# Feed-forward joints of a hybrid decoder layer: when the last rows' steps, operand loads, weight sums and next weights are issued

## The chip, the cores and the metric

The kernel runs on one NeuronCore of one Trainium2 chip. The metric is the device time of one execution in microseconds (us); less is better. In the profile PE is the matrix engine TensorE and PEld its weight loads, DVE is VectorE, ACT is ScalarE, POOL is GpSimd, and SP is the engine whose queue issues nearly all DMA transfers here.

## The reference

One decoder layer over a prompt of 2048 tokens and 8 x 8 sample tokens, D = 1024, D_FF = 4096, all in float32:

```python
h = rms_norm(x, g_mix_pre)                       # attention (window 128) and gated linear attention
mix = jnp.einsum('bte,ed->btd', jnp.concatenate([attn, gla_out], axis=-1), w_out)
x = x + rms_norm(mix, g_mix_post)
h = rms_norm(x, g_ffn_pre)
u = jax.nn.relu(jnp.einsum('btd,df->btf', h, w_up))
f = jnp.einsum('btf,fd->btd', u * u, w_down)
x = x + rms_norm(f, g_ffn_post)
```

The change concerns the last four lines, the feed-forward part, and its seams.

## The kernel before

**Numbers.** Every float32 operand is split into a high and a low part (`split_copy`, `split_by`: ACT writes the high part, DVE subtracts it from the source to get the low part), and each product is three matmuls (high x high, high x low, low x high).

**Feed-forward as seven products.** The prompt's 16 row tiles of 128 tokens form two superblocks (`sb` = 0, 1) of 8. Each matrix product is cut into quarters, and seven products of sums of quarters, numbered p = 1 to 7, take the place of eight. For `up` the sums of the tokens' quarters are the tensors H1 to H7 (from `ht`, kept in DRAM as `h_d`, loaded as `hraw`, split by `load_h`); the sums of w_up's quarters are made on the chip by DVE (`sums_13`, `sums_24`, tiles `t13`) and split (`split_sums`: `s130`, `s131`, `s240`, `s241`; `split_up`: `w00` to `w11`). For `down` the sums of the hidden quarters are stored in DRAM as `s_d`, and those of w_down are made during the first `up` by `sum_down` (four subtractions of 128x256 and a store to `t_d`).

**The stages.** After the out projection, whose last row tile (15) goes through `residual` (scale, add, second norm, transpose `xnT`, quarters' sums), come, for each superblock, `up(sb, fc)` for 16 chunks `fc` of 256 hidden columns, 7 products of 12 matmuls 128x512 each, and `down(sb)`: seven passes in the order `DOWN_ORDER`, each of 16 units of 12 matmuls. For `sb` = 0 products 0, 8 and 9 of each chunk are the sample's (`sam`, `both`, `fold`). In a unit, `down_operand` loads `rs` (from `s_d`) and `rt` (from `t_d` or w_down) and splits them into `o0s`, `o1s`, `o0t`, `o1t`; the raw tiles have two buffers, the split ones three. At a pass's end `gather` adds the four banks `dn` into the output tiles `f`, and at the end `finish` norms and stores a row tile.

**What sets the order.** `te`, `ac` and `dv` are in-order wrappers of PE, ACT and DVE: what is recorded through them (line L136) runs in the order of the code. Other instructions are placed among them by a scheduler. SP's queue is in order; a DMA there waits for its own semaphores and holds up all behind it. The first chunk has an order of its own, `UP_FIRST` = (1, 0, 2, 8, 5, 7, 9, 6, 3, 4); the others use `UP_ORDER` = (1, 5, 7, 0, 6, 3, 8, 2, 9, 4).

**Names and places.** "The first chunk" is (0, 0), the joint of out projection and feed-forward. Its operands H7, H6, H3, H4 are fetched one by one just ahead of their products:

```python
if first and p in H_LATE[1:]:
    if p != 7:
        fetch_h(0, p, "t" if p == 6 else "h")
    run(load_h(0, p))
```

`sum_down(fc - 1, 1)` stands behind product 1 of chunk `fc`, `sum_down(fc, 0)` behind the last product of chunk `fc`, and the last one, `sum_down(NFC - 1, 1)`, behind the last chunk. The weights of chunk (1, 0) are loaded and split after `down(0)`.

## Time and profile before

| | us |
|---|---|
| median of 3 runs (lowest, highest) | 2359.76 (2357.86, 2364.57) |
| profiled execution, its own time | 2353.07 |
| its span, first to last instruction | 2351.3 |
| PE busy in the span | 2245.4 |
| DVE busy | 1607.7 |
| ACT busy | 1202.8 |

The profiled execution lies 6.7 us below the median of the runs. PE is busy for 95% of the span, so that 106 us of it are time in which PE does nothing; 1.8 us of the profiled time lie outside the span. The granted clock of PE is 0.987 of full speed on the mean. Of an engine's row the last bracket is the idle time ahead of it and what ended that.

### The profile page before, as it was taken

To read this page: it belongs to the slowest core of one execution; us is meant where nothing else is said; L and a number is where in the kernel's file an instruction comes from. 1 tells how busy PE (TensorE), PEld (TensorE's weight loads), DVE (VectorE), ACT (ScalarE), POOL (GpSimd) and SP (SyncE) were. 2 spreads that over 40 slices of the span, in tenths; PEclk is the share of its full clock that TensorE was granted. 3 is DMA by queue.
4 is the path that set the end of the run, shared out by engine and by line. 5 is a ranking of instruction groups with operands and counts; after the bars stand their busy time and mean duration, and the time that the engine had idled before them with its cause. 6 is when DMAs were issued, how large, how long until landed. Compare 5 with 4: busy or idle time off the path is not lost.

```text
span 2351.3 us, 34131 instructions
## 1 busy us (share of the span) xinstructions
PE 2245.4 (95%) x11800; PEld 1885.6 (80%) x11800; DVE 1607.7 (68%) x3343; ACT 1202.8 (51%) x2513; POOL 271.5 (12%) x428
## 2 busy tenths in 40 slices
PE   8999999999999999889999999999989999999998
PEld 7888887888888788678888878888768888888886
DVE  5888868777777765677777765454676666545557
ACT  5787755345545444455555554333445555444444
POOL 3566412111121100000000000000000000000000
PEclk9999999999999999999999999999989999999999
DMA  6343231121112456676666786655744443666666
GB/s 226 125 147 120 97 115 46 64 70 50 46 46 90 141 178 207 208 262 232 233 236 241 245 287 215 190 177 162 241 141 150 150 150 146 217 223 191 195 194 213
DMA packets 226546, 391.86 MB, mean 167 GB/s; under 512 B 22865, under 2 KB 134886, under 8 KB 222262
## 3 DMA queue, kind: packets, MB, share of 16 engines
q1 hardware_dynamic: 226054, 389.56, 49.7%
q8 instruction: 93, 1.52, 0.3%
q14 instruction: 79, 0.65, 0.1%
q10 hardware_dynamic: 320, 0.13, 0.0%
HBM read 255.08 MB, written 135.59 MB: 166 GB/s over the span
## 4 chain that ended last, share of the span: by engine, by line
PE 69%; DVE 18%; ACT 5%; DMA 5%; issue 3%; POOL 1%; SPq 0%; DVEq 0%; ACTq 0%; POOLq 0%
PE dn L136 22%; PE uc L136 7%; PE ua L136 7%; PE out L1228 7%; PE gproj L136 5%; PE ue L136 4%; PE ud L136 4%; PE ub L136 3%; DVE AT L988 2%; DMA rt<-t_d 2%; DVE s L136 2%; DVE XQ L967 2%; PE proj L136 2%; DVE before L982 1%; PE sam L136 1%
## 5 line engine op out<-in xcount | busy, mean ns | idle before, releaser
L136 PE MATMUL dn<-o0t,o0s 128*128 128x512 f32 x896 | 352.1, 393 | 6.5 <-ACT o0t L222 6.0
L136 PE MATMUL dn<-o1t,o0s 128*128 128x512 f32 x896 | 353.5, 395 | 3.8 <-DVE o1t L223 3.5
L136 PE MATMUL dn<-o0t,o1s 128*128 128x512 f32 x896 | 351.9, 393 | 0.0
L223 DVE TENSOR_TENSOR o1s<-rs,o0s 128x512 fp32r<-128x512 f32 x224 | 154.7, 691 | 223.8 <-ACT o0s L222 211.8
L136 PE MATMUL gproj<-wg,gx 128*128 128x388 f32 x1408 | 288.5, 352 | 0.0
L222 ACT ACTIVATE o0s<-rs 128x512 fp32r<-128x512 f32 x224 | 141.3, 631 | 282.1 <-PE dn L136 236.1
L136 PEld LDWEIGHTS gproj<-wg,gx 128*128 128x128 f32 x1408 | 245.0, 190 | 8.6 <-issue 4.5
L136 PEld LDWEIGHTS dn<-o0t,o0s 128*128 128x128 f32 x896 | 168.9, 189 | 47.0 <-ACT o0t L222 9.4
L136 PEld LDWEIGHTS dn<-o1t,o0s 128*128 128x128 f32 x896 | 168.9, 189 | 46.2 <-DVE o1t L223 9.6
L136 ACT ACTIVATE st<-st 128x512 f32<-128x512 f32 x224 | 141.1, 630 | 123.1 <-DVE st L136 119.1
L136 PE MATMUL uc<-H,s 128*128 128x512 f32 x768 | 194.4, 401 | 9.9 <-ACT s L1423 8.8
L136 PEld LDWEIGHTS dn<-o0t,o1s 128*128 128x128 f32 x896 | 169.1, 189 | 35.4
L136 PE MATMUL ua<-H,w 128*128 128x512 f32 x744 | 184.1, 396 | 6.7 <-ACT w L1423 4.3
L223 DVE TENSOR_TENSOR o1t<-rt,o0t 128x512 fp32r<-128x512 f32 x224 | 153.8, 687 | 49.0 <-ACT o0t L222 48.6
L136 PEld LDWEIGHTS uc<-H,s 128*128 128x128 f32 x768 | 146.3, 191 | 47.6 <-ACT s L1423 9.6
L222 ACT ACTIVATE o0t<-rt 128x512 fp32r<-128x512 f32 x224 | 139.3, 622 | 66.2 <-DMA rt<-t_d 40.7
L136 PEld LDWEIGHTS ua<-H,w 128*128 128x128 f32 x744 | 140.6, 191 | 38.9 <-ACT w L1423 5.1
L1228 PE MATMUL out<-wo,mt 128*128 128x512 f32 x680 | 160.9, 395 | 0.2 <-DVE x L1359 0.2
L212 POOL TENSOR_TENSOR frs<-rs_v,half 128x1 f32<-128x1 f32 (+1 forms) x13 | 8.9, 698 | 1311.7 <-DVE rs_v L210 726.4
L1228 PEld LDWEIGHTS out<-wo,mt 128*128 128x128 f32 x680 | 126.5, 188 | 28.8 <-DVE x L1359 0.6
L136 DVE TENSOR_TENSOR st<-st 128x512 f32<-128x512 f32 x160 | 110.8, 692 | 54.9 <-ACT st L136 51.6
L136 PE MATMUL proj<-wa_hi,xh 128*128 128x384 f32 (+1 forms) x272 | 96.1, 357 | 0.6 <-ACT wa_hi L136 0.6
(368 smaller groups left out, 4283.6 us busy)
## 6 DMA issues: line engine op xcount, KB each, us to landing
s_d<-st SPq DMA_DIRECT2D x32, 1792.0 KB, 9.1
rs<-s_d SPq DMA_DIRECT2D x224, 256.0 KB, 2.8
raw<-in_w_up SPq DMA_DIRECT2D x64, 512.0 KB, 5.1
rt<-t_d SPq DMA_DIRECT2D x128, 256.0 KB, 3.2
rt<-in_w_down SPq DMA_DIRECT2D x96, 256.0 KB, 3.0
t<-in_w_down SPq DMA_DIRECT2D x64, 256.0 KB, 3.7
t_d<-t SPq DMA_DIRECT2D x32, 512.0 KB, 8.1
gx<-xt_d SPq DMA_DIRECT2D x28, 512.0 KB, 4.3
```

Source lines behind the costliest of these rows:

```text
L136: ins = call(*a, **k)
L212: nc.gpsimd.tensor_tensor(out, v[:n], e, op=ALU.pow)
L222: nc.scalar.activation(hi, src, AF.Copy)
L223: vector.tensor_tensor(lo, src, f32(hi), op=ALU.subtract)
L967: nc.vector.tensor_tensor(xq[rr, :, l, r, : n // 2].rearrange("p g (m b) -> p g m b", b=b), dr[rr], qr[rr], op=ALU.mult)
L982: nc.vector.tensor_tensor(br, br, bl[..., b - 1 :].to_broadcast(list(br.shape)), op=ALU.add)
L988: nc.vector.copy_predicated(dst, m, gm.rearrange("p h (m b) -> p h m b", b=b))
L1228: te.matmul(p_, x, w[:, cc], start=k + u == 0, stop=k == KT - 1 and u == len(products) - 1)
```

## The change

Nothing is computed in another way except that `down` takes its passes in another order, with the additions in `gather` to match (as many as before). The rest is when things are issued:

- The last row tile's `residual` is a generator, `last_rows`, whose steps run between the products of the first chunk, and each operand load has a fixed place there (`opening`). `s130` and `s131` of the first chunk are made before that tile's steps, the w_up loads of chunk (0, 1) go out at once, and the tile's `xnT` transposes and its four `ht` subtractions move behind products 7 and 6. A pool `keep` on the left side lets those tiles share memory with later ones.
- `sum_down` runs twice in a chunk from chunk 2 on, behind products 1 and 2, and a third time (behind product 4) in chunks 4, 6, 8 and 10, so that none is left behind the last chunk.
- In `down(0)` the loads of the second superblock's H are in the first three and a half passes; `finish` of the first four row tiles comes one pass earlier; at the start of the last pass the weights of chunk (1, 0) are loaded, summed and split (`ahead_of_up`); `finish` of the other four row tiles runs inside chunks (1, 0) and (1, 1).

```diff
-DOWN_ORDER = (6, 1, 5, 7, 2, 3, 4)
-H_EARLY, H_LATE = (1, 2), (5, 7, 6, 3, 4)
+DOWN_ORDER = (6, 1, 5, 3, 2, 7, 4)
+DOWN_SUMS = (4, 6, 8, 10)
+H_FETCH = ((6, 0), (6, 8), (1, 0), (1, 8), (5, 0), (5, 8), (3, 0))
+H_EARLY, H_LATE = (1, 2), (5, 7, 6, 4, 3)
...
-    def residual(i, banks, vector=nc.vector):
+    def residual(i, banks, tensor=nc.tensor, scalar=nc.scalar, vector=nc.vector):
...
+        def ahead(kind):
+
+            if last:
+                return
+            if kind == "a":
+                split_up(sb, fc + 1, 0, ac, dv)
+            elif kind in ("13", "24"):
+                split_sums(sb, fc + 1, int(kind), ac, dv)
+            else:
+                (sums_13 if kind == "s13" else sums_24)(sb, fc + 1, dv)
+
+        def downs(p):
+
+            if sb == 0 and fc > 1 and p in ((1, 2, 4) if fc in DOWN_SUMS else (1, 2)):
+                sum_down(*next(down_halves))
...
+    def opening(p, taken, ahead):
+
+        if p == 1:
+            taken(p)
+            split_sums(0, 0, 13, ac, dv)
+        elif p == 0:
+            next(last_rows)
+        elif p == 2:
+            taken(p)
+            next(last_rows)
+            fetch_h(0, 3, "t")
+        elif p == 8:
+            taken(p)
+            run(load_h(0, 7, ac, dv))
+            fetch_h(0, 6, "tmp")
+        elif p == 5:
+            taken(p)
+            sums_24(0, 0, dv)
+            split_sums(0, 0, 24, ac, dv)
+            fetch_h(0, 4, "raw")
+            run(load_h(0, 6, ac, dv))
+            U.pop("tmp").release()
+        elif p == 7:
+            taken(p)
+            next(last_rows)
+        elif p == 9:
+            taken(p)
+            close_pools(R)
+            for q in H_LATE[3:]:
+                h_pools[q] = open_pool(f"h_{q}")
+            run(load_h(0, 3, ac, dv))
+        elif p == 6:
+            run(load_h(0, 4, ac, dv))
+            ahead("a")
+            taken(p)
+            run(last_rows)
             load_up(0, 2)
             for half in range(2):
                 load_down(0, half)
-        if sb == 0:
-            sum_down(fc, 0)
-        dv.tensor_tensor(s[:, 6], s[:, 0], s[:, 6], op=ALU.subtract)
-        dv.tensor_tensor(s[:, 5], s[:, 3], s[:, 6], op=ALU.subtract)
-        dv.tensor_tensor(s[:, 4], s[:, 5], s[:, 0], op=ALU.add)
-        if sb == 0:
-            sample_features(fc, sam)
-
-        def end():
-            dv.tensor_tensor(s[:, 1], s[:, 1], V, op=ALU.add)
-            yield
-            squared(s[:, 1])
-            dv.tensor_tensor(s[:, 2], s[:, 1], s[:, 5], op=ALU.subtract)
-            nc.sync.dma_start(s_d[sb][fc], s)
-
-        return end()
+        elif p == 3:
+            ahead("s13")
+            ahead("13")
+        else:
+            ahead("s24")
+            ahead("24")
...
-                if sb == 0 and not first:
-                    sum_down(fc - 1, 1)
...
-        if sb == 0:
-            sum_down(fc, 0)
...
+    def ahead_of_up():
+
+        open_pools(U, ("ah", "al", "t13", "s13h", "s13l", "s24h", "s24l"), "u1")
+        load_up(1, 0)
+        yield 1.4
+        split_up(1, 0, 0)
+        yield 0.7
+        sums_13(1, 0, nc.vector)
+        yield 1.4
+        split_sums(1, 0, 13, nc.scalar, nc.vector)
+        yield 1.3
+        sums_24(1, 0, nc.vector)
+        yield 1.4
+        split_sums(1, 0, 24, nc.scalar, nc.vector)
+        yield 1.3
...
+            if (sb, p, fc) == (0, late, 0):
+                deque(chain.from_iterable(todo), 0)
+                for name in ("fa", "smp", "fs"):
+                    Dp.pop(name).release()
+                weights = ahead_of_up()
+                next(weights)
+                todo.extend((*waiting, weights))
...
-                if p == 3 and sb == 0:
-                    todo.append(finish(NB, f[NB]))
-                if p == 3 or p == late:
-                    todo.extend(finish(i, f[i]) for i in range(sb * 8 + 4 * (p == late), sb * 8 + 4 * (p == late) + 4))
-                if p == 3 and sb == 1:
+                if p == 2:
+                    if sb == 0:
+                        todo.append(finish(NB, f[NB]))
+                    todo.extend(finish(i, f[i]) for i in range(sb * 8, sb * 8 + 4))
...
+    last_rows = residual(*early.pop(0), te, ac, dv)
+    sums_13(0, 0, dv)
+    run(load_h(0, 5, ac, dv))
+    load_up(0, 1)
+    next(last_rows)
     for sb in range(NSB):
...
-            load_up(sb, 0)
-            split_up(sb, 0, 0)
-        sums_13(sb, 0, nc.vector)
-        split_sums(sb, 0, 13, nc.scalar, nc.vector)
-        sums_24(sb, 0, nc.vector)
-        split_sums(sb, 0, 24, nc.scalar, nc.vector)
-        if sb:
-            split_up(sb, 0, 1)
-        load_up(sb, 1)
-        end = iter(())
+            open_pools(U, ("raw", "bh", "bl", "st0"), "u1")
+            load_up(sb, 1)
+        end, ends = iter(()), iter(())
         for fc in range(NFC):
-            end = up(sb, fc, end)
+            if sb and fc < 2:
+                ends = chain.from_iterable(rows_left[2 * fc : 2 * fc + 2])
+            if sb and fc == 1:
+                Dp.pop("fbA").release()
+                open_pools(U, ("st1",), "u1", "right")
+            end = up(sb, fc, end, ends)
+            run(ends)
```

The first place is DVE in the first chunk. `ht_11` is the last rows' sum tile, `st_0_0` the first chunk's hidden quarters, `H31`, `H61`, `H41` are low parts of operands, `s131_0_1` and `w01_0_1` low parts of the next chunk's weights. Before:

```order
L136 TENSOR_TENSOR ht_11_11026<-ht_11_11026 128x512
L223 TENSOR_TENSOR H31_0_11281<-hraw_0_3_0_11276,H30_0_11280 128x1024
L1424 TENSOR_TENSOR s131_0_0_11139<-t13_0_0_11135,s130_0_0_11138 128x1024
L223 TENSOR_TENSOR H31_0_11281<-hraw_0_3_2_11278,H30_0_11280 128x1024
L1469 TENSOR_TENSOR t13_0_0_11135<-t13_0_0_11135,raw0_0_0_10812 128x4x128
L1470 TENSOR_TENSOR t13_0_0_11135<-raw1_0_0_10813,t13_0_0_11135 128x4x128
L1424 TENSOR_TENSOR s241_0_0_11145<-t13_0_0_11135,s240_0_0_11144 128x1024
L136 TENSOR_TENSOR t13_0_1_11171<-raw0_0_1_11148,raw1_0_1_11149 128x4x128
L136 TENSOR_TENSOR t13_0_1_11171<-raw0_0_1_11148 128x4x128
L136 TENSOR_TENSOR w01_0_1_11183<-raw0_0_1_11148,w00_0_1_11182 128x1024
L136 TENSOR_TENSOR st_0_0_11152<-st_0_0_11152,ud_0_0_11156 128x512
L136 TENSOR_TENSOR s131_0_1_11243<-t13_0_1_11171,s130_0_1_11242 128x1024
```

After:

```order
L138 TENSOR_TENSOR H31_0_11248<-hraw_0_3_0_11158,H30_0_11247 128x1024
L138 TENSOR_TENSOR H31_0_11248<-hraw_0_3_2_11160,H30_0_11247 128x1024
L138 TENSOR_TENSOR H41_0_11266<-hraw_0_4_0_11201,H40_0_11265 128x1024
L138 TENSOR_TENSOR H41_0_11266<-hraw_0_4_2_11203,H40_0_11265 128x1024
L138 TENSOR_TENSOR w01_0_1_11272<-raw0_0_1_11089,w00_0_1_11271 128x1024
L138 TENSOR_TENSOR st_0_0_11121<-st_0_0_11121,ua_0_0_11106 128x512
L138 TENSOR_TENSOR st_0_0_11121<-st_0_0_11121 128x512
L138 TENSOR_TENSOR ht_11_11026<-ht_11_11026 128x512 x4
L138 TENSOR_TENSOR st_0_0_11121<-st_0_0_11121,uc_0_0_11105 128x512
L138 TENSOR_TENSOR t13_0_1_11307<-raw0_0_1_11089,raw1_0_1_11090 128x4x128
L138 TENSOR_TENSOR t13_0_1_11307<-raw0_0_1_11089 128x4x128
L138 TENSOR_TENSOR s131_0_1_11311<-t13_0_1_11307,s130_0_1_11310 128x1024
```

The `ht` subtractions have gone from ahead of the first chunk's weights to a place between H4's split and the next chunk's sums; the next chunk's `s131_0_1` now stands behind H6, H3, H4, `w01_0_1` and them.

The second place is SP's queue at the end of the first `up`. `t_d15_147<-t_15_1` is the store of w_down's last sums, `rs_0_6_n` and `rt_0_6_n` the operands of unit n of the first down pass, `s_d0_15` the last chunk's store. Before:

```order
L1621 DMA rs_0_6_3_14128<-s_d0_3_103 128x512
L1621 DMA rt_0_6_3_14134<-t_d3_135 128x512
L1397 DMA hraw_1_5_2_14487<-h_d1_99 128x1024
L1607 DMA sm_d_148<-samp_15_13991 128x256
L1621 DMA rs_0_6_4_14152<-s_d0_4_104 128x512
L1621 DMA rt_0_6_4_14158<-t_d4_136 128x512
L1589 DMA s_d0_15_115<-st_0_15_13843 128x3584
L1500 DMA t_d15_147<-t_15_1_13876 512x1x256
L1621 DMA rs_0_6_5_14176<-s_d0_5_105 128x512
```

After:

```order
L1414 DMA hraw_1_7_0_14508<-h_d1_99 128x1024
L1515 DMA t_d15_147<-t_15_1_13821 512x1x256
L1718 DMA rs_0_6_2_14113<-s_d0_2_102 128x512
L1718 DMA rt_0_6_2_14119<-t_d2_134 128x512
L1718 DMA rs_0_6_3_14137<-s_d0_3_103 128x512
L1718 DMA rt_0_6_3_14143<-t_d3_135 128x512
L1704 DMA sm_d_148<-samp_15_13993 128x256
L1785 DMA smp_0_0_14315<-sm_d_148 128x8x128
L1718 DMA rs_0_6_4_14161<-s_d0_4_104 128x512
L1718 DMA rt_0_6_4_14167<-t_d4_136 128x512
L1640 DMA s_d0_15_115<-st_0_15_13874 128x3584
L1718 DMA rs_0_6_5_14185<-s_d0_5_105 128x512
```

That store has moved from just ahead of unit 5's operands to ahead of unit 2's; half a load of sample features (`smp_0_0`) has come in ahead of unit 4's.

The third place is DVE at the end of `down(0)`. `t13_1_0`, `s131_1_0` and `s241_1_0` are the sums of chunk (1, 0)'s weights and their low parts; `f_4` to `f_7` are output tiles of `finish`. Before, behind the last pass:

```order
L210 TENSOR_SCALAR rs_v_17101<-fssq_4_17097 128x1
L1424 TENSOR_TENSOR w01_1_0_17196<-raw0_1_0_17191,w00_1_0_17195 128x512
L1651 SCALAR_TENSOR_TENSOR f_4_14472<-f_4_14472,frs_4_17100,gfpost0_14058 128x1024
L210 TENSOR_SCALAR rs_v_17113<-fssq_5_17109 128x1
L210 TENSOR_SCALAR rs_v_17125<-fssq_6_17121 128x1
L1632 TENSOR_TENSOR f_4_14472<-f_4_14472,fx1_4_17095 128x1024
L1651 SCALAR_TENSOR_TENSOR f_5_14474<-f_5_14474,frs_5_17112,gfpost0_14058 128x1024
L1651 SCALAR_TENSOR_TENSOR f_6_14476<-f_6_14476,frs_6_17124,gfpost0_14058 128x1024
L210 TENSOR_SCALAR rs_v_17137<-fssq_7_17133 128x1
L1462 TENSOR_TENSOR t13_1_0_17199<-raw0_1_0_17191,raw1_1_0_17192 128x4x128
L1651 SCALAR_TENSOR_TENSOR f_7_14478<-f_7_14478,frs_7_17136,gfpost0_14058 128x1024
L1424 TENSOR_TENSOR s131_1_0_17203<-t13_1_0_17199,s130_1_0_17202 128x1024
```

After, at the seam of the last two passes (units (7, 13) to (4, 0)):

```order
L225 TENSOR_TENSOR o1t_0_7_13_16634<-rt_0_7_13_16632,o0t_0_7_13_16633 128x512
L225 TENSOR_TENSOR o1s_0_7_14_16652<-rs_0_7_14_16650,o0s_0_7_14_16651 128x512
L225 TENSOR_TENSOR o1t_0_7_14_16658<-rt_0_7_14_16656,o0t_0_7_14_16657 128x512
L1439 TENSOR_TENSOR s131_1_0_16914<-t13_1_0_16886,s130_1_0_16913 128x1024
L1484 TENSOR_TENSOR t13_1_0_16886<-t13_1_0_16886,raw0_1_0_16750 128x4x128
L225 TENSOR_TENSOR o1s_0_7_15_16676<-rs_0_7_15_16674,o0s_0_7_15_16675 128x512
L225 TENSOR_TENSOR o1t_0_7_15_16682<-rt_0_7_15_16680,o0t_0_7_15_16681 128x512
L225 TENSOR_TENSOR o1s_0_4_0_16700<-rs_0_4_0_16698,o0s_0_4_0_16699 128x512
L1485 TENSOR_TENSOR t13_1_0_16886<-raw1_1_0_16751,t13_1_0_16886 128x4x128
L225 TENSOR_TENSOR o1t_0_4_0_16706<-rt_0_4_0_16704,o0t_0_4_0_16705 128x512
```

The sums and the low part `s131_1_0` now stand among the operand splits some 16 units before the end of `down(0)`, no longer behind the `finish` of four row tiles.

## Rows read from the trace of the kernel before

**Rows 1.** The page, part 1: busy us (share of the span) and instructions of each engine.

```profile
PE 2245.4 (95%) x11800; PEld 1885.6 (80%) x11800; DVE 1607.7 (68%) x3343; ACT 1202.8 (51%) x2513; POOL 271.5 (12%) x428
```

**Rows 2.** Windows: length, then busy us (instructions) of PE, PEld, DVE, ACT, POOL; PEclk, DMA share, GB/s.

```profile
976.00:1021.00 45.00, 30.01 (x123) 23.34 (x122) 32.30 (x42) 22.93 (x34) 1.44 (x2) 0.77 0.83 267
...
1021.00:1043.00 22.00, 22.00 (x106) 18.26 (x105) 19.72 (x33) 11.79 (x21) 0.00 (x0) 1.00 0.72 249
...
1350.00:1375.00 25.00, 19.70 (x73) 14.72 (x72) 14.29 (x25) 11.40 (x21) 0.00 (x0) 0.86 0.92 308
...
1640.00:1674.00 34.00, 33.02 (x144) 26.69 (x142) 24.05 (x36) 19.36 (x33) 2.50 (x4) 1.00 0.61 194
...
1696.00:1740.00 44.00, 33.11 (x114) 24.36 (x113) 30.55 (x41) 17.15 (x26) 3.67 (x4) 0.84 0.47 156
```

**Rows 3.** Timeline of PE around the first chunk: start, us, group, idle before and releaser.

```profile
983.44 1.11 PE L136 MATMUL sam<-w,xsT 128*128 128x256 f32 x8
...
987.27 1.15 PE L1375 MATMUL xnT<-ident,x 128*128 128x128 f32 x8 [2.72 <-DVE x L136]
...
993.69 1.22 PE L136 MATMUL uc<-H,s 128*128 128x512 f32 x2 [5.27 <-ACT s L1423]
...
1006.18 1.11 PE L136 MATMUL sam<-fold,both 128*128 128x64 f32 x4 [4.02 <-ACT both L136]
...
1023.74 0.63 PE L136 MATMUL uc<-H,s 128*128 128x512 f32 x2
```

**Rows 4.** Timeline of ACT, SP's queue and DVE in the first chunk.

```profile
991.33 1.06 ACT L222 ACTIVATE H<-hraw 128x1024 fp32r<-128x1024 f32 x1 [1.42 <-DMA hraw<-h_d]
...
1003.65 1.06 ACT L136 ACTIVATE w<-raw 128x1024 fp32r<-128x1024 f32 x1 [4.62 <-DMA raw<-in_w_up]
...
984.99 2.48 SPq L1397 DMA_DIRECT2D hraw<-h_d  x2
...
997.19 2.71 SPq L1420 DMA_DIRECT2D raw<-in_w_up  x2
...
1005.15 0.69 DVE L136 TENSOR_TENSOR t<-raw,raw 128x512 f32<-128x512 f32 x1 [4.86 <-DMA raw<-in_w_up]
...
1006.36 1.22 DVE L136 TENSOR_TENSOR w<-raw,w 128x1024 fp32r<-128x1024 f32 x1
```

**Rows 5.** Timeline of DVE, SP's queue and PE at the start of the first down pass.

```profile
1360.23 0.42 DVE L136 TENSOR_TENSOR t<-t 128x256 f32<-128x256 f32 x1
...
1360.67 0.57 SPq L1500 DMA_DIRECT2D t_d<-t  x1
...
1361.30 0.73 SPq L1621 DMA_DIRECT2D rs<-s_d  x1
...
1368.55 0.80 PE L136 MATMUL dn<-o0t,o0s 128*128 128x512 f32 x1 [4.45 <-ACT o0t L222]
...
1374.02 0.40 PE L136 MATMUL dn<-o0t,o0s 128*128 128x512 f32 x1
```

**Rows 6.** Timeline of PE from the last down pass into the second up.

```profile
1702.40 0.74 PE L136 MATMUL ua<-H,w 128*128 128x512 f32 x2 [0.22 <-ACT w L1423]
...
1705.02 4.09 PE L136 MATMUL ua<-H,w 128*128 128x512 f32 x10 [1.88 <-DVE w L1424]
...
1712.67 1.22 PE L136 MATMUL uc<-H,s 128*128 128x512 f32 x2 [3.56 <-ACT s L1423]
...
1731.36 0.73 PE L136 MATMUL ua<-H,w 128*128 128x512 f32 x2 [4.05 <-ACT w L1423]
...
1739.21 2.90 PE L136 MATMUL ua<-H,w 128*128 128x512 f32 x12
...
1758.69 1.54 PE L136 MATMUL ua<-H,w 128*128 128x512 f32 x6
```

**Rows 7.** Timeline of PE in the last down pass, unit 7.

```profile
1674.35 0.50 PE L136 MATMUL dn<-o1t,o0s 128*128 128x512 f32 x1 [1.32 <-DVE o1t L223]
```

**Rows 8.** The page, part 6: a store of w_down's sums, median us to landing.

```profile
t_d<-t SPq DMA_DIRECT2D x32, 512.0 KB, 8.1
```

More of the change, by code (lines that the diff above doesn't have):

```diff
@@ L238, in three @@
         engine.matmul(ps, lh, rl, start=False, stop=False)
-        engine.matmul(ps, ll, rh, start=False, stop=last)
+        return engine.matmul(ps, ll, rh, start=False, stop=last)
     gcol = cpool.tile([P, KT], F32, name="gcol")
@@ L1506, in squared, with up, s, product @@
         ac.activation(t, t, AF.Square)
[L1508 to L1514 removed]
+    def up(sb, fc, before, steps=iter(())):
+        first, last = (sb, fc) == (0, 0), fc == NFC - 1
         X, Z, Y, V = (bank([P, BT], kind, f"u{kind}_{sb}_{fc}") for kind in ("ab"[first], "c", "ba"[first], "de"[fc % 2]))
         sam = bank([P, BT], "b", f"sam_{fc}") if sb == 0 else None
+        place = []
+        def s(n):
+            if not place:
+                pool = keep if (sb, fc % 2) == (0, 1) else U[f"st{fc % 2}"]
+                place.append(pool.tile([P, 7, BT], F32, tag="st", name=f"st_{sb}_{fc}", bufs=1))
+            return place[0][:, n]
+        def product(p):
+            out = {1: X, 2: X, 5: Z, 3: Z, 7: V, 4: V, 6: Y}[p]
+            hi, lo = H[p]
+            for k in range(KT // 2):
+                for u, (a, b) in enumerate(((0, hi), (0, lo), (1, hi))):
+                    te.matmul(
+                        out, weight(sb, fc, p, a, k), b[:, k], start=p in (1, 5, 7, 6) and k + u == 0,
+                        stop=k == KT // 2 - 1 and u == 2, skip_group_check=True,
+                    )
+        def add(out, a, b, op=ALU.add):
+            dv.tensor_tensor(s(out), a, b, op=op)
+        def taken(p):
+            if p == 1:
+                ac.activation(s(1), X, AF.Copy)
+            elif p == 5:
+                ac.activation(s(3), Z, AF.Copy)
+            elif p == 7:
+                add(3, s(3), V)
+            elif p == 6:
+                add(1, s(1), Y)
+                add(3, s(3), s(1))
+                squared(s(3))
+            elif p == 2:
+                squared(s(0), X)
+            elif p == 8:
+                both.append(U["sam"].tile([P, FC], F32, tag="sam", name=f"both_{fc}", bufs=1))
+                ac.activation(both[0], sam[:, :FC], AF.Copy)
+            elif p == 9:
+                for u in range(2):
+                    te.matmul(
+                        sam[:, FC + u * NS : FC + (u + 1) * NS], both[0][:, u * P : (u + 1) * P], fold, start=True, stop=True
+                    )
+        both = []
+        def ahead(kind):
[10 more added lines that the diff above has]
+                sum_down(*next(down_halves))
@@ L1712, in gather @@
             yield 0.7
-        elif p == 3:
-            add(fa[:, two], fa[:, two], p_)
-            yield 0.7
+        elif p == 7:
+            for dd in (two, one):
+                add(fb[:, dd], fb[:, dd], p_)
+                yield 0.7
         else:
@@ L1777, in down @@
             del parts[n]
-            if n == NFC // 2 and sb == 0:
-                smp = load_sample(0)
-            if fc == 8 and sb == 0:
-                todo.append(load_h(1, H_ORDER[DOWN_ORDER.index(p)]))
+            if n == 8:
+                with tc.issue_after(done.ins):
+                    for part in range(2 * (sb == 0)):
+                        load_sample(0, part)
+                    gains_post(sb)
+            if p == 5 and sb == 0 and fc in (8, NFC - 1):
+                load_sample(1, fc // 9)
```

238 lines of the change are left out of this document (129 added, 109 removed).

## The prediction

> **What bounds the kernel now.** I read the busy times first: PE works in 95% of the span, DVE in 68% and ACT in 51% [rows 1]. The sum of PE's work is not touched by this change, so only the 106 us in which PE stands still, and the time in which it runs at less than full clock, can be had. Then I read the windows by stage. In a steady chunk of the first up PE is busy throughout (22.00 of 22.00), with DVE at 19.72 [rows 2]. Three stretches are different: the first chunk with 30.01 of 45.00, the start of the first down pass with 19.70 of 25.00, and the way from the last down pass into the second up with 33.11 of 44.00; together 15.0 + 5.3 + 10.9 = 31.2 us idle. In each the granted clock also drops, to 0.77, 0.86 and 0.84 on the mean [rows 2]. [...] Last, PE's timeline says who ended each wait there.
>
> A product of 12 matmuls takes 19.48 / 7 = 2.78 us (seven of them between 1739.21 and 1758.69) [rows 6]. After the wait of 4.45 us one unit of 12 took 1374.02 - 1368.55 = 5.47 us [rows 5]. So a wait is paid again, by 2.7 us, where the clock has fallen during it.
>
> **First chunk.** From the end of the sample's second product (984.55) to the second product of chunk (0, 1) at 1023.74 lie 39.2 us [rows 3]. Full-clock work in it: five products and one of the next chunk, 16.7 us, transposes 1.15, the fold some 0.4: 18.2 us. So 21.0 us are lost. The long waits: 2.72 for the last rows' norm on DVE, 5.27 for `s130` on ACT, 4.02 for `both` on ACT [rows 3]. The last is a queue: `both` stood behind a weight split that had waited 4.62 us for w_up loads, issued only at 997.19 [rows 4].
>
> The change makes `s130` and `s131` ahead of the last rows' steps, so product 5 follows without a wait, and issues those w_up loads at the start, so that `both` has nothing late ahead of it. What is late next? DVE. I follow its new order (first place in the change). The last rows' norm ended at about 987.2 (the transposes begin then); one more low part (1.22) now stands ahead of it: 988.4. H7's low parts follow, 2 x 1.22, to 990.9, so product 7 waits some 3 us. H6's two loads share H7's memory and go out as H7's halves are split, the first at about 989.7. A load of this kind issued at 984.99 was first used at 991.33, 6.3 us later; with ACT's 1.06 H6's first low part starts at 997.1 [rows 4]. From there DVE is a chain without a gap: H6 2.44, one hidden sum 0.69, H3 2.44, H4 2.44, `w01_0_1` 1.22, two sums 1.38, four `ht` subtractions 2.76, one sum 0.69, two weight sums 1.38, ACT's `s130_0_1` 1.06, `s131_0_1` 1.22: 17.7 us (1.22 for 1024 columns, 0.69 for 512 [rows 4]). It ends at 1014.8, where the third matmul of chunk (0, 1)'s second product needs it; before, that matmul ran at about 1024.2. Gain: 9.4 us, not 21. Upper bound: back to back these additions start 0.61 apart (1005.15 and two of them to 1006.36), a tenth off the DVE part: 11.1. Lower bound: the products behind H6 are three, and one of the next chunk; at the low clock each takes 5.47, so 997.3 + 21.9 = 1019.2, gain 5.0. I take 9.4, because with two of the four at low clock PE is done at 997.3 + 16.5 = 1013.8, still ahead of DVE.
>
> [...]
>
> **Start of the first down pass.** PE waits 4.45 us for unit 5's operands, whose load left SP at 1361.30, right behind the store of w_down's last sums at 1360.67, and that waited for DVE's last sum, begun at 1360.23 [rows 5]. In the new order (second place) this store is ahead of unit 2's loads, its sums having been made within chunk 15. Unit 5's load then waits for its buffer, that is for unit 3's split, which needs unit 0 to be through. Counting back five units from the stop at 1364.1 the pass begins at about 1349.3 (the other 0.85 us of idle time taken off); unit 0 ends at 1352.1, splits follow, issue near 1354. Even with the 8.1 us of a store [rows 8] a load issued then lands by 1362.1, a little before it must be split. Gain 4.45 + 2.7 = 7.2. Bounds: 0 if another transfer takes the place of the store, 8.0 with the 0.85.
>
> The price is paid in the chunks: 32 `sum_down` of 4 x 0.42 us are only moved, none is added [rows 5]. Four chunks have three instead of two: 19.72 + 1.7 = 21.4 of 22 us on DVE, still covered. Each store must land (8.1 [rows 8]) before the next load into that half may pass SP: three make 24.3 us in a chunk of 22, two make 16.2 in the next, so a delay of some 2 us is caught up. I take 0; if it were not caught up, 4 x 2.3 = 9.
>
> **Into the second up.** Chunk (1, 0) runs from 1702.40 to 1739.21, 36.8 us, where a chunk takes 19.48: 17.3 lost, with waits of 1.88 for DVE's `w01`, 3.56 for ACT's `s130` and 4.05 for ACT's `w10` [rows 6]. All of them are weights loaded after the pass and split behind the `finish` of four row tiles. Now sums and splits are made in the last two passes (third place); only `w10` and `w11` remain, needed five products later, 14 us. What is late next is chunk (1, 1): its loads leave at the end of the pass, and DVE has four gathers 2.8, five sums of 512 columns 3.5, two low parts and six full-row steps of `finish` 9.8, and half a `w01` 0.7 before chunk (1, 1) can start: 16.8 us, begun 2 us ahead of the pass's end, against 19.5. Covered by some 4 us; I still take 1 us off for the waits on GpSimd between these steps: 16.3. If that cover is gone, PE waits and the clock falls once more: 16.3 - 4 - 2.7 = 9.6 as lower bound.
>
> The cost lies in the pass before the last. DVE works 24.05 of 34.00 us in a stretch of the old last pass in which four row tiles are finished [rows 2], and there PE once waited 1.32 us for a split [rows 7]. The same finish now comes a pass earlier, with four weight sums, a half `w01` and a low part between: 2.8 + 0.7 + 1.2 = 4.7 us more. The old stall goes, a new one comes: between +1.3 (it just fits) and -4.7 + 1.3 = -3.4 (nothing fits); I take -1.
>
> **Sum.** 9.4 + 7.2 + 16.3 - 1 = 31.9 us off the profiled execution's 2353.07: 2321.2. The median of the runs shown is 6.7 us above that execution, so 2327.9, about 2328, and by the bounds of the terms 2322 (11.1 + 8.0 + 17.3 + 1.3 = 37.7) to 2349 (5.0 + 0 + 9.6 - 3.4 = 11.2). Less than 0.3%, 7.1 us, is not to be told from no change.
>
> **The rivals.**
>
> *The first chunk keeps the low clock* (chance 0.14): gaps of 1 to 3 us remain ahead of products 7 and 6. For it speaks the 0.77 of the stretch, against it that DVE and not PE ends last there. Gain 5.0 or nothing in place of 9.4: 2332 to 2337.
>
> *DVE becomes the bound in the last two passes and chunk (1, 0)* (0.12): 9.6 - 3.4 in place of 15.3: 2337. For it speaks the 1.32; against it the fewer `finish` steps in the last pass.
>
> *The joint of the first down pass does not open* (0.08): unit 5 waits for its load as before, behind half a load of sample features and the last chunk's store; gain 0 there: 2335.
>
> *Slower* (0.05): in the first up `sum_down` now stands in DVE's in-order queue ahead of the next chunk's low parts. If the loads it waits for come late through SP, DVE stands as it once stood 4.86 us for w_up [rows 4]; it has 2.3 us to spare in a chunk. In 14 chunks that is 14 x 2.6 = 36 us, which just eats the gain; from 5.2 us of waiting on (2.9 lost a chunk, 40) the kernel is slower by more than 0.3%, at 7 us 2394. Against it: a half's store and next load are a whole chunk apart, 22 us for 8.1 and a load.
>
> *No change* (0.05): the waits only move, as that 36 would make them.
>
> The forecast has the remaining 0.56; its own range is 2322 to 2335. Faster by over 0.3%: 0.56 + 0.14 + 0.12 + 0.08 = 0.90, less 0.02 for the case that the three rivals meet with a wait in every chunk: 0.88; with half of that each, same 0.06 and slower 0.06. The range that should hold 8 in 10 goes from 2315 (all upper bounds, or the runs' median 6.7 us nearer to the profiled execution than before, and both in part) to 2346 (two of the rivals together; beyond it lie the sum of all lower bounds, no change and slower).
>
> **What would show it.** Right: product 5 of the first chunk without a wait on `s130`; the first down pass without a wait of over 1 us and clock 1.00; chunk (1, 0) in about 20 us; DVE busiest in the sixth pass. Wrong: a granted clock of 0.50 from product 7 through chunk (0, 1); waits of PE on DVE's splits of over 2 us in the sixth pass; PE waiting once in every chunk of the first up.

## The result, and the profile after

The changed kernel takes 2321.13 us (median of 5 runs, 2317.98 to 2325.82) where the kernel before takes 2359.75 (5 runs, 2352.02 to 2364.57). The ratio is 0.9846, with a 95% interval from 0.9829 to 0.9863: faster by 38.6 us. The forecast of 2328 with its range from 2315 to 2346 holds. The profiled execution has a span of 2316.2 us against 2351.3, so 35.1 us less, where the sum of the terms was 31.9. That the two are close is partly luck, as the table shows.

The page of the changed kernel, part 1 (busy us, share of the span, instructions), answers to [rows 1]. The instructions of each engine are as many as before, yet PE is busy 19.3 us less:

```profile
PE 2226.1 (96%) x11800; PEld 1881.0 (81%) x11800; DVE 1606.9 (69%) x3343; ACT 1197.0 (52%) x2513; POOL 271.1 (12%) x428
```

Windows of the changed kernel at the places of [rows 2]: the first chunk, a steady chunk of the first up, the start of the first down pass, its sixth pass, the way into the second up, and a steady chunk there (length, then busy us of PE, PEld, DVE, ACT, POOL; PEclk, DMA share, GB/s):

```profile
975.00:1020.00 45.00, 35.63 (x157) 28.12 (x156) 34.88 (x44) 24.70 (x38) 1.90 (x2) 0.92 0.76 242
1041.62:1063.15 21.53, 21.53 (x105) 18.11 (x104) 16.41 (x27) 11.41 (x18) 0.00 (x0) 1.00 0.60 214
1342.00:1367.00 25.00, 21.94 (x94) 17.14 (x93) 13.35 (x21) 11.26 (x19) 0.00 (x0) 1.00 0.93 314
1592.00:1626.00 34.00, 32.24 (x134) 25.99 (x133) 28.54 (x42) 19.83 (x33) 3.36 (x5) 0.95 0.73 225
1683.00:1727.00 44.00, 44.00 (x194) 36.05 (x194) 33.43 (x46) 20.10 (x31) 2.97 (x4) 1.00 0.53 180
1711.82:1731.04 19.22, 19.22 (x85) 15.75 (x84) 14.84 (x20) 10.07 (x15) 0.00 (x0) 1.00 0.60 211
```

The way into the second up has no idle time left (44.00 of 44.00), the first chunk has 9.4 us idle in place of 15.0, the start of the down pass 3.1 in place of 5.3. The sixth pass, which the prediction feared for, has a granted clock of 0.95. And one line answers to no term of the sum: a steady chunk of the second up, with PE busy throughout before and after, takes 19.22 us where it took 19.48 [rows 6].

PE's timeline of the changed kernel around the first chunk (start, us, group, idle before and releaser), against [rows 3]:

```profile
982.35 1.11 PE L138 MATMUL sam<-w,xsT 128*128 128x256 f32 x8
983.30 2.91 PE L138 MATMUL uc<-H,s 128*128 128x512 f32 x12
988.45 0.50 PE L138 MATMUL ud<-H,s 128*128 128x512 f32 x1 [2.23 <-ACT H L138]
...
998.09 0.79 PE L138 MATMUL ua<-H,s 128*128 128x512 f32 x1 [4.28 <-ACT H L138]
...
1013.96 0.73 PE L138 MATMUL uc<-H,s 128*128 128x512 f32 x2 [1.10 <-ACT s L138]
1015.22 2.56 PE L138 MATMUL uc<-H,s 128*128 128x512 f32 x10 [0.53 <-DVE s L138]
...
1034.00 0.66 PE L138 MATMUL sam<-fold,both 128*128 128x64 f32 x4 [3.04 <-ACT both L138]
1034.47 4.58 PE L138 MATMUL ue<-H,w 128*128 128x512 f32 x12
...
1041.62 0.62 PE L138 MATMUL uc<-H,s 128*128 128x512 f32 x2
```

Product 5 follows the sample's product without a wait, product 7 waits for H7 and product 6 for H6's load, as forecast. New is the wait at 1034.00, one chunk later, with a product of 4.58 us behind it, over which the granted clock was 0.63 (1034.47 to 1039.05 us).

VectorE's timeline of the changed kernel in these two chunks: H6's low parts, the low part `s131` that the third matmul at 1015.22 waits for, and the sum of product `ub` of chunk (0, 1):

```profile
998.07 2.50 DVE L138 TENSOR_TENSOR H<-hraw,H 128x1024 fp32r<-128x1024 f32 x2 [3.60 <-ACT H L138]
...
1013.93 1.23 DVE L138 TENSOR_TENSOR s<-t,s 128x1024 fp32r<-128x1024 f32 x1 [1.12 <-ACT s L138]
...
1028.61 0.68 DVE L138 TENSOR_TENSOR st<-st,ub 128x512 f32<-128x512 f32 x1
```

PE's timeline of the changed kernel in the first down pass and its sixth pass, against [rows 5, 7]:

```profile
1357.34 0.49 PE L138 MATMUL dn<-o0t,o0s 128*128 128x512 f32 x1 [2.40 <-ACT o0t L224]
...
1617.95 0.50 PE L138 MATMUL dn<-o1t,o0s 128*128 128x512 f32 x1 [1.75 <-DVE o1t L225]
```

The wait of 2.40 us is for unit 5's operands. SP's queue and ScalarE of the changed kernel show the last chunk's store (`s_d`), unit 5's two loads right behind it, and their first use:

```profile
1347.26 0.32 SPq L1640 DMA_DIRECT2D s_d<-st  x1
1347.86 0.32 SPq L1718 DMA_DIRECT2D rs<-s_d  x1
1348.46 1.47 SPq L1718 DMA_DIRECT2D rt<-t_d  x1
...
1355.69 0.63 ACT L224 ACTIVATE o0s<-rs 128x512 fp32r<-128x512 f32 x1 [4.43 <-DMA rs<-s_d]
```

The stretches of both profiled executions, between starts of PE's rows, with the forecast beside them (us):

| from, to | before | after | gain | forecast |
|---|---|---|---|---|
| start, first product of chunk (0, 0) | 976.9 | 975.8 | 1.1 | 0 |
| to the second product of (0, 1) | 46.9 | 38.2 | 8.7 | 9.4 |
| to the second product of (0, 2) | 21.9 | 27.7 | -5.8 | 0 |
| to the first down pass | 303.1 | 298.8 | 4.3 | 0 |
| to chunk (1, 0) | 353.7 | 349.4 | 4.3 | 7.2 - 1 |
| to the second product of (1, 1) | 39.5 | 22.0 | 17.6 | 16.3 |
| to the second down pass | 289.5 | 285.6 | 3.9 | 0 |
| to the end | 319.9 | 318.8 | 1.1 | 0 |

Three forecast terms are there in their order of size. Lines that were to be zero are not: chunk (0, 1) lost 5.8 us, and the steady chunks of both ups gained some 8 (4.3 and 3.9), with nothing to wait for before or after.

### The profile page after: what moved, and what is told of

Its sections match the earlier page's. It is cut to its first block, busy times and chain, and to the rows that moved or that the text cites. A ratio compares the mean times of both kernels' runs of the same rounds, so it can differ in the third digit from the quotient of the medians.

```text
span 2316.2 us, 34119 instructions
## 1 busy us (share of the span) xinstructions
PE 2226.1 (96%) x11800; PEld 1881.0 (81%) x11800; DVE 1606.9 (69%) x3343; ACT 1197.0 (52%) x2513; POOL 271.1 (12%) x428
## 4 chain that ended last, share of the span: by engine, by line
PE 64%; DVE 18%; ACT 6%; DMA 6%; issue 5%; POOL 1%; ACTq 0%; SPq 0%; DVEq 0%; POOLq 0%
PE dn L138 20%; PE out L1230 7%; PE ua L138 7%; PE uc L138 7%; DMA rt<-t_d 4%; PE gproj L138 4%; PE ud L138 4%; PE ub L138 3%; PE ue L138 3%; DVE AT L990 2%; DVE s L138 2%; DVE XQ L969 2%; PE proj L138 2%; DVE before L984 2%; PE sam L138 1%
## 5 line engine op out<-in xcount | busy, mean ns | idle before, releaser
L138 PE MATMUL uc<-H,s 128*128 128x512 f32 x768 | 187.5, 392 | 1.7 <-ACT s L138 1.1
L138 PE MATMUL ua<-H,w 128*128 128x512 f32 x744 | 179.2, 390 | 0.0
L138 ACT ACTIVATE s<-t 128x1024 fp32r<-128x1024 f32 x62 | 65.8, 1061 | 93.9 <-PE ud L138 29.0
```

Of the source, the lines that this page charges most:

```text
L138: ins = call(*a, **k)
```

## The experiments

Times vary by a few us from execution to execution for a reason outside the change: from the start to the first product of chunk (0, 0), the profiles of the kernels below took 975.1 to 984.2 us, on nearly the same instructions. The granted clock shows where: in that stretch it stood at 0.50 for 17 us in the changed kernel's profile and for 38 in the longest ones (`samples_later`, `before_placed`); over the whole profiled executions it was 0.992 in the former, 0.987 and 0.980 in the latter. So small effects are read from the stretches of the table, and the medians stand beside them.

**`both` copied early.**

```
                 ac.activation(both[0], sam[:, :FC], AF.Copy)
+                if held:
+                    squared(s(3))
+                    ahead("24")
+                    squared(s(6))
...
-        both = []
+        both, held = [], (sb, fc) == (0, 1)
```

> The changed kernel, but in chunk (0, 1) alone ScalarE copies `both` ahead of the two squares of `st` and the split of `s24` that it stood behind. Theory: `both` was late because ScalarE's queue stood behind squares that waited for VectorE. Then the wait of 3.04 us before the fold of chunk (0, 1) is under 0.5, the product behind it takes 2.9 us in place of 4.58, and the second product of chunk (0, 2) comes 4 to 5 us earlier after that of chunk (0, 1) (27.66 us becomes 22.7 to 23.7). Rival: VectorE itself is late, and the next product that needs it waits instead: a new wait of 2 us or more before chunk (0, 2) is through, and under 1.5 us gained.

Median 2317.68, ratio 0.9833 (0.981 to 0.9857). The stretch from (0, 1) to (0, 2) takes 22.8 us in place of 27.7, so 4.9 are back; three runs below that leave this place as it is took 26.1, so that 3.3 is the least. ScalarE's timeline of the changed kernel and PE's of this one show why:

```profile
1030.05 1.29 ACT L138 ACTIVATE st<-st 128x512 f32<-128x512 f32 x2 [2.80 <-DVE st L138]
1031.44 1.06 ACT L138 ACTIVATE s<-t 128x1024 fp32r<-128x1024 f32 x1
1032.40 1.27 ACT L138 ACTIVATE st<-st 128x512 f32<-128x512 f32 x2
1033.58 0.36 ACT L138 ACTIVATE both<-sam 128x256 f32<-128x256 f32 x1
```

```profile
1035.65 0.55 PE L138 MATMUL sam<-fold,both 128*128 128x64 f32 x4
1036.01 3.00 PE L138 MATMUL ue<-H,w 128*128 128x512 f32 x12
```

The queue theory holds: `both` could have been copied when the sample's product ended at 1028.2, and stood behind squares of `st` that VectorE delivered late (the 2.80).

**The subtractions last, too.**

```
         elif p == 6:
...
-            run(last_rows)
...
         else:
             ahead("s24")
             ahead("24")
+            run(last_rows)
```

> The changed kernel with `both` of chunk (0, 1) copied early, as in the run of that name, and the last rows' four subtractions of `ht` (2.74 us of VectorE) at the end of the first chunk's steps, behind the next chunk's weight sums and low parts in place of ahead of them. Theory: VectorE is the chain that sets the end of the first chunk, so the second product of chunk (0, 1) comes 1.5 us earlier (38.17 us from the chunk's start becomes 36 to 37), and the stretch behind it stays at 22 to 23.5 us. Rival: the subtractions are only paid later: a new wait in chunk (0, 1) takes the 1.5 us back.

Median 2322.83, ratio 0.985 (0.9828 to 0.9872). To the second product of (0, 1) it is 36.8 us, where the changed kernel took 38.2 and the runs with the same first chunk 37.4 to 37.9. So VectorE does end last there, and 0.5 to 1.3 us are gained. But the next stretch is 30.0 us. PE's timeline of this kernel, and ScalarE's:

```profile
1029.11 3.36 PE L138 MATMUL uc<-H,s 128*128 128x512 f32 x7 [6.55 <-ACT st L138]
```

```profile
1027.97 0.60 ACT L138 ACTIVATE st<-ua 128x512 f32<-128x512 f32 x1 [4.25 <-DMA h_d<-ht]
```

The rival holds, and for a reason that neither theory named: `st` of chunk (0, 1) takes the memory of `ht`, so ScalarE cannot copy into it before the subtractions and their store are through.

**The last sum of w_down late again.**

```
-DOWN_SUMS = (4, 6, 8, 10)
+DOWN_SUMS = (4, 6, 8)
...
+            sum_down(*next(down_halves))    # behind chunk 15
```

> The changed kernel with one of the four third sums moved back: the last half of w_down's sums is made and stored behind chunk 15, as in the kernel before. Theory: the store of these sums ahead of the loads is what made the old wait of 4.45 us. Then the longest wait in the first units of the first down pass grows from 2.40 to 4 or 5 us, the granted clock falls behind it, and the pass is 3 to 5 us longer. Rival: the wait that is left after the change is the loads' own, behind the store of the last chunk's `st`, and the sums' store adds little: a wait of 2 to 3 us, no low clock, under 1 us lost.

Median 2329.68, ratio 0.9893 (0.9869 to 0.9917). The seven passes of `down(0)` take 356.5 us, 7.1 more:

```profile
1365.44 0.80 PE L138 MATMUL dn<-o0t,o0s 128*128 128x512 f32 x1 [6.63 <-ACT o0t L224]
```

The theory holds, and is under its size (4 or 5 us of waiting, 3 to 5 lost). Of the 7.1, 5.8 lie in the first 30 us of them: waits and slow matmuls are 10.5 us there and 4.8 in the changed kernel. The rest are waits further on.

**The sample's loads later.**

```
-                with tc.issue_after(done.ins):
+                with tc.issue_after(ended[0].ins):    # unit 9's last load
```

> The changed kernel with the two loads of the sample's features (512 KB each) and of the gains queued on SP behind unit 9's loads in the first down pass; they stood between the loads of units 3 and 7. Theory: what is left of the first down pass's wait (2.40 us for unit 5's operands) is DMA traffic in front of unit 5's load: these 1 MB and the 1.8 MB of the last chunk's store of `st`. Then the wait is under 1 us and 1.5 to 3 us are gained in the pass. Rival: the load waits for its buffer, a chain of load, ScalarE and VectorE that is too slow by itself: 2 to 3 us of waiting as now, or the wait only moves to units 10 and 11, behind the moved loads.

Median 2330.46, ratio 0.9885 (0.9866 to 0.9903); `down(0)` takes 354.1 us, 4.7 more. PE's timeline there:

```profile
1364.75 0.50 PE L138 MATMUL dn<-o0t,o0s 128*128 128x512 f32 x1 [1.96 <-ACT o0t L224]
...
1383.50 0.80 PE L138 MATMUL dn<-o0t,o0s 128*128 128x512 f32 x1 [2.71 <-ACT o0t L224]
```

Unit 5 waits 1.96 in place of 2.40, and a second wait has come, in unit 10, behind the moved loads. That is what the rival says, but the theory was not put to the test. SP's queue of this kernel has loads of the second superblock's H, 512 KB each as the sample's were, in the two places that these left, the first of them again ahead of unit 5's load:

```profile
1351.55 0.43 SPq L1414 DMA_DIRECT2D hraw<-h_d  x1
...
1355.62 0.32 SPq L1718 DMA_DIRECT2D rs<-s_d  x1
```

So the traffic ahead of that load is the same. Which of it, of the store of `st` and of the two buffers of `rs` sets what is left stays open.

**The second up's weights late, three ways.** First only in the written order:

```
-                next(weights)
-                todo.extend((*waiting, weights))
+                todo.extend(waiting)
...
+            deque(weights, 0)    # behind the last down pass
```

> The changed kernel, but the weights of chunk (1, 0) are loaded and made behind the last down pass; the finish of four row tiles stays inside the first two chunks. Theory: the loss before the change was the weights' lateness. Then chunk (1, 0) takes 30 to 37 us in place of 19.2 (a load of some 4.4 us, a split, sums, each waited for, with the clock fallen), 10 to 17 us lost. Rival: it was the finish of the four row tiles that stood in the way, and weights alone cost one load: under 6 us lost.

Median 2319.04, ratio 0.9842 (0.9813 to 0.9871); 22.0 us to (1, 1), nothing lost. VectorE's timeline of this kernel shows a low part and the later sums some 50 us ahead of the pass's end (chunk (1, 0) starts at 1694.2), as in the changed kernel (1639.59 against 1689.84):

```profile
1644.15 1.22 DVE L1439 TENSOR_TENSOR s<-t,s 128x1024 fp32r<-128x1024 f32 x1
1645.40 0.69 DVE L1484 TENSOR_TENSOR t<-t,raw 128x512 f32<-128x512 f32 x1
```

The scheduler had moved them forward again. So where the step is written is not what opens this joint; that it is the place of the weights in memory, which is free by then, is argued and was not tested by itself. The order was now tied down:

```
...
+        if sb == 0:
+            with tc.issue_after(ended[0].ins), tc.issue_after(ended[1].ins):
+                deque(ahead_of_up(), 0)    # last load of the pass, last add
```

> The changed kernel, with the loads of the weights of chunk (1, 0) queued on SP behind the last unit's loads of the down pass, and their sums and low parts queued on VectorE behind the pass's last additions. (In the run before this one they were only written later in the program; the scheduler moved them forward again, and the loss was 0.) Theory: late weights make TensorE wait; with loads that are there when the pass ends, it waits for w01, s130 and s131 behind one finish step: chunk (1, 0) takes 23 to 26 us in place of 19.2, 4 to 7 us lost. Rival 1: the old 17.3 us come back whole (36 us), since what counts is the order behind the pass. Rival 2: nothing is lost, and the old loss was the loads' alone.

Median 2324.21, ratio 0.9856 (0.9832 to 0.9879); 26.0 us to (1, 1), 4.0 lost, in waits of 0.92 for w01, 1.27 for s131 and 0.66 for s241. Then the finish in front of them:

```
+            deque(chain.from_iterable(finish(4 + j, f[4 + j]) for j in range(4)), 0)
             with tc.issue_after(ended[0].ins), tc.issue_after(ended[1].ins):
```

> The run `weights_held` (loads of the weights of chunk (1, 0) behind the last unit's, sums and low parts behind the pass), and now the finish of the last four row tiles stands on VectorE ahead of those sums, whole, in place of inside the first two chunks. In the kernel before its steps and the sums alternated, so this is the far end of that order. `weights_held` alone cost 4.0 us. Theory: the old 17.3 us were mainly the finish in front of the splits, whose steps wait for a load of `fx` each (about 6 us a row in the sixth pass): chunk (1, 0) takes 36 to 44 us in place of 26.0. Rival: the finish is short beside the pass's end and the old loss was the loads alone: 26 to 30 us.

Median 2343.1, ratio 0.9954 (0.9937 to 0.997); 47.2 us to (1, 1), 25.2 lost. VectorE's timeline and PE's:

```profile
1698.44 1.23 DVE L1729 TENSOR_TENSOR f<-f,fx 128x1024 f32<-128x1024 f32 x1
1704.42 1.23 DVE L1729 TENSOR_TENSOR f<-f,fx 128x1024 f32<-128x1024 f32 x1 [4.75 <-DMA fx<-x_d]
1710.45 1.23 DVE L1729 TENSOR_TENSOR f<-f,fx 128x1024 f32<-128x1024 f32 x1 [4.80 <-DMA fx<-x_d]
1711.59 0.69 DVE L1439 TENSOR_TENSOR w<-raw,w 128x512 fp32r<-128x512 f32 x1
```

```profile
1712.33 2.07 PE L138 MATMUL ua<-H,w 128*128 128x512 f32 x4 [22.42 <-DVE w L1439]
```

The two ends, 4.0 and 25.2, enclose the old 17.6: the last two row tiles' sums wait 4.8 us each for the one buffer of `fx`, and whatever stands behind them on VectorE waits along. The theory holds, at 3 us over its upper figure (47.2 against 44).

**Why are steady chunks shorter?** In the trace, matmuls of 512 columns start 233.3 ns after each other in some products and 226.7 in others, at a granted clock of 1.00. The first guess was the place in a partition:

```
-            open_pools(U, ("st0", "s24h", "s24l", "raw", "ah", "al", "s13h", "s13l", "t13", "bh", "bl", "st1"), "u1")
+            open_pools(U, ("st0", "st1", "raw", "t13", "ah", "al", "bh", "bl", "pad", "s13h", "s13l", "s24h", "s24l"), "u1")
+            U["pad"].tile([P, 4848], F32, tag="pad", name="pad", bufs=1)
```

> The kernel before, with nothing changed but the addresses in the second up: the weight sums s13 and s24 lie 131 to 147 KB into a partition in place of 73 to 101. No instruction is added, left out or moved. Theory: the interval between matmuls (233.3 ns in one set of products, 226.6 in another, at the same granted clock) goes by the addresses of moving operand and weights. Then products 5, 7, 6 and 3 go at 226.6 ns, a chunk of the second up takes 19.1 to 19.2 us in place of 19.48, and 4.5 to 5.5 us are gained in all, 0.2%. Rival: the interval goes by what else runs (order of the engines' work, DMA), or is a state of the execution: 19.48 as before.

Median 2361.31, ratio 1.0016 (1.0001 to 1.0031). A window of a steady chunk:

```profile
1765.09:1784.28 19.19, 19.19 (x85) 15.76 (x84) 12.78 (x17) 9.81 (x15) 0.00 (x0) 1.00 0.42 150
```

The chunk is at 19.19 as the theory has it. The time is not, because the new layout also ties the first operand splits of `down(1)` to memory in use. PE waits 9.78 us for them, and ScalarE for the last chunk's store:

```profile
2040.32 1.15 ACT L222 ACTIVATE o0t<-rt 128x512 fp32r<-128x512 f32 x2 [6.50 <-DMA s_d<-st]
```

So addresses matter, but which property of them? TensorE alone, over the whole partition:

> A kernel that leaves out the whole layer (its outputs are zeros): TensorE alone, 96 matmuls and then 156 sets of 24 (128x128 weights, 512 moving columns, float32r, the pattern hi, lo, hi of the kernel's products), each set with another pair of places in a partition: moving operand at 13 places from 20 KB to 217 KB, weights at 12 places from 28 KB to 209 KB, 16 KB apart. No other engine works, no DMA runs. Theory: the interval between matmuls is 226.6 or 233.3 ns and goes by the two places alone: 233 where the moving operand lies above about 128 KB and the weights below it, 226.6 in the other three quarters. Rival: one interval for all sets, so that the two levels of the kernels come from other engines or DMA.

All 156 sets take 226.7 ns, for instance these two (24 matmuls, 5.44 us from start to start):

```profile
204.81 5.60 PE L23 MATMUL mb_wl<-big 128*128 128x512 f32 x24
210.25 5.60 PE L23 MATMUL mc_wa<-big 128*128 128x512 f32 x24
```

High or low is not it, and that theory falls. Every place there was a multiple of 256 bytes; in the kernels the left pools start 32 bytes past one and the right pools 224.

> As the run `grid`, TensorE alone and the layer left out, but the places differ in small steps: moving operand and weights start 0, 32, 64, ... 224 bytes past a multiple of 256 (8 by 8 sets of 24 matmuls with both low in the partition; 4 by 4 sets with either or both high). In `grid` every place was a multiple of 128 bytes, and all 156 sets went at 226.7 ns. In the kernels the products at 227 ns have both operands at the same start within 128 bytes (32 and 32, or 96 and 96), those at 233.3 ns have 96 for the moving operand and 32 for the weights. Theory: the interval is 226.7 ns where the two starts are equal within 128 bytes, and more where they differ. Rival 1: one of the two starts alone decides, whatever the other is. Rival 2: 226.7 ns in all sets, so that the higher level of the kernels needs other engines or DMA beside it.

The timeline of TensorE, in which the letter behind `m` and `w` is the start of the moving operand and of the weights in steps of 32 bytes (a is 0, b is 32):

```profile
78.81 5.61 PE L21 MATMUL Ama_wa<-big 128*128 128x512 f32 x24
84.25 5.75 PE L21 MATMUL Ama_wb<-big 128*128 128x512 f32 x24
89.84 5.76 PE L21 MATMUL Ama_wc<-big 128*128 128x512 f32 x24
...
123.36 5.77 PE L21 MATMUL Amb_wa<-big 128*128 128x512 f32 x24
128.96 5.64 PE L21 MATMUL Amb_wb<-big 128*128 128x512 f32 x24
134.44 5.75 PE L21 MATMUL Amb_wc<-big 128*128 128x512 f32 x24
```

Of these sets, equal starts take 5.44 to 5.48 us to the next one, unequal ones 5.59 to 5.61. As means of the 23 intervals of a set, 226.7 ns stand at equal starts alone (16 of 20 sets; the other four have 227.8 to 228.4); everything else is at 232.4 to 234.0, but 228.7 to 229.4 where the moving operand starts 64 bytes further. The theory holds with 256 in place of 128 bytes. Now the same in the kernels:

```
     ident = cpool.tile([P, P], F32, name="ident")
+    cpool.tile([P, 48], F32, name="pad")
```

> The kernel before, with one unused tile of 192 bytes in a partition at the front of SBUF and nothing else changed: every tile that is laid from the left starts 192 bytes later, so that left and right tiles start at the same place within 256 bytes (224; it was 32 on the left and 224 on the right). Theory, from the run `starts` (226.7 ns between matmuls where moving operand and weights start at the same place within 256 bytes, 228.9 to 234.3 where not): the 1920 products' matmuls at 233.4 ns and the 1344 of the down passes at 230.6 go at 226.7, so a chunk of the second up takes 19.05 us in place of 19.48, one of the first up 21.4 in place of 21.85, and 15 to 19 us are gained in all: 2339 to 2343, ratio 0.992 to 0.9935. Then about 11 us of what the change brought is this, too. Rival: in the full kernel other engines or DMA hold the interval up, and the chunks stay within 0.1 us of 19.48 and 21.85.

> The changed kernel with the same 192 bytes at the front and with `both` of chunk (0, 1) copied early. Theory: a chunk of the second up 19.05 us in place of 19.22, of the first 21.4 in place of 21.53, the down passes 2 to 3 us less in all, and the 4.9 us of `both`: 10 to 12 us under the changed kernel, 2309 to 2312, ratio to the kernel before 0.979 to 0.981. Rival: most of the first up's interval is already at 226.7 ns in the changed kernel and only the 4.9 us show: 2316.

The kernel before with the pad: median 2341.2, ratio 0.9944 (0.9926 to 0.9962), span 2336.3. The changed kernel with the pad and `both` early: median 2315.65, ratio 0.9832 (0.9809 to 0.9855), span 2304.5. Windows of steady chunks in the first and second up, first those of before with the pad, then of the changed kernel with it:

```profile
1065.87:1087.36 21.49, 21.49 (x105) 18.13 (x104) 16.75 (x27) 11.43 (x18) 0.00 (x0) 1.00 0.72 236
1753.54:1772.58 19.04, 19.04 (x86) 15.77 (x84) 12.78 (x17) 9.82 (x15) 0.00 (x0) 1.00 0.44 151
```

```profile
1057.07:1078.57 21.50, 21.50 (x106) 18.13 (x104) 16.75 (x27) 11.42 (x18) 0.00 (x0) 1.00 0.70 238
1721.83:1740.87 19.04, 19.04 (x85) 15.77 (x84) 13.58 (x19) 9.36 (x14) 0.00 (x0) 1.00 0.42 151
```

With equal starts both kernels have the same chunks, 21.5 and 19.04 us, as the theory has it. Its time holds for the kernel before (2339 to 2343). For the last kernel it was 2309 to 2312, and the median lies above it, at the rival's 2316; the chunks and the span, 11.7 us under the changed kernel's, speak for the theory. Before, 5 of 7 products of a chunk had unequal starts (operands H on the right, weights on the left); after, one of 7 in the first up and two in the second. The pad takes 13.9 us off the kernel before. The last kernel has the shortest span of all; its median is below the changed kernel's 2321.13, but their intervals overlap.

## Why the prediction was right, and where it was not

- **First chunk, 9.4 forecast, 8.7 measured.** VectorE's chain from H6 on was to take 17.7 us; it runs from 998.07 to 1015.16, 17.1 us, and ends last: the third matmul starts at 1015.22, and taking the subtractions out of the chain's way brought 0.5 to 1.3 us. Counted to that matmul, as the prediction did, the gain is 7.9. The waits before products 7 and 6 (2.23 + 0.76 and 4.28 + 0.47) are the forecast ones.
- **The step that failed here** is the word "ends". The sum stopped at the second product of chunk (0, 1), as if VectorE were then level with TensorE. It was 4.4 us behind: it took up the sum of product `ub` at 1028.61, which PE had ended at 1024.2, where a steady chunk's follows within 0.1 us. And `both` stood in ScalarE's queue behind what VectorE still owed: 5.8 us of the 8.7 went back in the next chunk, and 2.9 of the forecast 9.4 are left. The old kernel's `both` wait was named in the prediction as "a queue"; the same queue one chunk on was not looked at.
- **The rival of the low clock** does not hold as a whole: 0.92 over the first 45 us where it was 0.77. Its gain of 5.0 put four products behind H6's load at 5.47 us each, as one unit had taken behind the wait of 4.45. The clock did fall behind the gap of 4.28, to 0.50 from 998.0 to 1004.8 us, and behind the 3.04, to 0.50 from 1035.5 to 1038.9; but between the two it was at 1.00 (1004.8 to 1035.5), and of the four products only the first ran slow (5.06 us for 11 of its matmuls; the others 3.21, 2.88 and 2.88 for 12). The measured 8.7 (7.9 to the third matmul) speaks against the 5.0. With the next chunk the net 2.9 is under 5.0 too, but there the wait for `both` took 3.04 and the slow product behind it some 1.7.
- **First down pass, 7.2 forecast.** Added over the starts of all matmuls, waits and slow matmuls of its first 30 us fall from 8.8 to 4.8, so some 4. The store does cost here (5.8 in that stretch when one half came back). The mis-sized step is "splits follow, issue near 1354", 4.7 us into the pass. Unit 5's loads left SP at 1347.86 and 1348.46, 7.4 and 8.0 us into it (it starts at 1340.42), as soon as unit 3's low parts were through; unit 3's load, issued at 1340.07, had first been used at 1345.88, which the prediction gave no time. From issue to first use unit 5's loads took 7.8 and 8.2 us, about the 8.1 that were allowed, behind the last chunk's store; so they came 2.40 us too late. Some 3 of the 7.2 us went to the rival that the joint does not open, and one sign of being right failed: no wait of over 1 us was to be left.
- **Sums in the chunks, 0 forecast, 0 found.** Chunk (0, 4) with three sums takes 21.52 us and (0, 2) with two 21.53. The rival that ends slower falls with it: no wait of PE stands in any later chunk of the first up. A store of sums also lands in 3.3 us and not in the 8.1 of [rows 8].
- **Sixth pass, -1 forecast.** A wait of 1.75 in place of 1.32, and this time the clock fell behind it (0.79 from 1616 to 1624 us): -2.3 over the rest of `down(0)`, within -3.4 to 1.3. VectorE is busier there than in the old last pass, 28.54 of 34 us against 24.05, but PE waits for it for long only this once.
- **Second up, 16.3 forecast, 17.6 measured,** the upper bound. The cover of 4 us for chunk (1, 1) held whole. The mechanism, weights behind the finish, is the one that `weights_held` and `finish_first` bracket. That their place in the program would decide is not borne out: in `weights_late` the scheduler moved them forward, and nothing was lost.
- **The sentence that was wrong:** "The sum of PE's work is not touched by this change." It fell by about 11 us: 14 chunks of the first up at 0.32, 15 of the second at 0.26, and 2.5 in `down(0)`. The instructions are the same; the pools of weights and operands changed sides, and with that the starts of their tiles. This paid for the 5.8 lost in chunk (0, 1) and the 3 lost in the down pass, and made the sum of 31.9 look better than its terms: without these 11 us the profiled gain would be some 24.

## What to carry to other kernels

When a critical engine has caught up at one instruction, ask how far behind the engines feeding it still are, and what is queued there for the next stage; a gain at a joint is only booked when the backlog is gone (5.8 of 8.7 us went back here). Count the time per instruction in stretches without any wait, before and after: here some products went from 233.3 ns a matmul to 226.7 because the layout of memory had moved, and that was a gain to be had by itself (192 unused bytes gave the kernel before a third of what this change gave). And where a scheduler orders the work, the place where a step is written may not matter at all (0 lost in `weights_late`); look in the trace where it went, also before calling a moved load a test.
